# Two blocks of a top-k threshold search pass from a search on VectorE and ScalarE to one on ScalarE alone

## The chip, the cores and the metric

The kernel runs on one core of one Trainium2 chip. Its time is the device time of one execution in microseconds (us). The profile is of one execution and counts from the first instruction to the last (the span). Of the core's engines the text names TensorE (PE: matmuls; PEld: the loading of their weights), VectorE (DVE), ScalarE (ACT), GpSimd (POOL) and SyncE (SP), which issues most DMAs. PE, ACT, DVE, POOL and SP each take their own instructions in order.

## What is computed

One decoder layer on 1024 tokens of width 1024. Two branches read the same projection: an RWKV-7 recurrence (8 heads of 64) and a sparse attention in which an indexer picks for each query the 256 keys with the highest score. Their outputs are gated, added to the input, and followed by a SwiGLU block. The change is in the part that picks the keys:

```python
def one_block(args):                       # 8 blocks of 128 queries
    ...
    sc = jax.nn.relu(einsum('bqhd,bsd->bqhs', qib, k_idx))
    score = einsum('bqhs,bqh->bqs', sc, wib) * idx_scale
    score = jnp.where(causal, score, -jnp.inf)
    _, sel = lax.top_k(score, topk)        # topk = 256
    ...
    prob = jax.nn.softmax(logits_of_selected, axis=-1)
```

Block b has (b+1)*128 keys that a query may see. Blocks 0 and 1 see at most 256, so nothing is picked there. Blocks 2 to 7 have 384, 512, 640, 768, 896 and 1024 keys.

## The kernel before

**Order of work.** PE's instructions keep the order in which the program is written; those of the other engines are put in order when the kernel is built, earlier lines first where several could start, and later lines wherever an engine would else be idle. `fill` is a queue of generators of matmul work; `pump(n)` takes about n matmuls from it, and so the text of the program says which matmuls of the fill lie between those of the main work. `ticks(n, m)` spreads n such matmuls over m equal parts and takes one step of the generator `beside` after each part.

**Stages.** First the projections of the indexer, then `scores`: for each of blocks 2 to 7 the products on PE, a rectification on ACT (L970) and a weighted sum on DVE. Beside this and the first search PE takes the projections of the RWKV and attention inputs from `fill`. Then comes `rwkv` for four quarters q = 0 to 3 of 256 tokens. Beside q = 0 PE takes the projection of V and half of the gates, beside q = 1 the attention of blocks 0 to 3 (`attend(0)`) and the other gates, beside q = 2 and 3 the merge and the FFN of the first half of the tokens. After `rwkv` follows `attend(1)` for blocks 4 to 7, with the rest of the first half's FFN as fill, and then the second half's merge and FFN.

**The search.** `image` turns the scores into integers with the same order (L986, L987). `select` then finds for each query the 256th highest value by bisection: 16 steps on the upper 16 bits, a preparation (L1040 on ACT, L1042 on DVE, in pieces of up to 512), and 16 steps on the rest. Each step counts, for each block, how many values reach the threshold. A block is counted either on DVE (`is_ge` with a sum, L1015) or on ACT (`Sign` with a sum, L1018); the first `nv` of its `order` are DVE's. With `nv` above 0 the thresholds are moved by three small DVE instructions for all blocks together (L1020 to L1022), and with `nv` = 0 by two small ACT instructions for each block (L1026, L1027). At the end each block gets a mask `bias[b]`: a `Sign` on ACT (L1056), six DVE instructions (L1057 to L1062), and a copy on ACT (L1063).

There are two searches. The first is written behind the scores and handles blocks 5, 2 (DVE) and 4, 3 (ACT). The second (`LATE`, blocks 7 and 6, `nv` = 0) is the generator `beside`: its 16 steps, preparation, 16 steps and two masks make 35 steps, which `ticks` takes in 14, 4, 9 and 6 during the quarters of `rwkv` and in 2 at the end. The scores of `LATE` blocks are kept in tiles `kept` of their own (4 bytes a value), and their masks are written into the same memory; the other blocks have a mask tile of 2 bytes a value and scores in a pool that is closed before `rwkv`. The second search writes its unused result to `junkl`, the first to `junk`. In the second search the preparation and the masks take `tmp` tiles, of which there are four, in turn with everybody else: two for a mask, one for a piece of the preparation.

**Weights.** A weight tile is loaded by DMA into one of three `wst` tiles (from SP's queue, and during `rwkv` from ACT's), then split into a high part on ACT (L116) and a low part on DVE (L117), and multiplied in three terms (L149, L150, L154).

**GpSimd.** It issues the loads of q = 0 of `rwkv` (L566), those of `attend` (L1077 to L1105), and a few late ones. [...]

## Time and profile before

| what | value |
|---|---|
| median of 3 runs | 1708.05 us (1706.07 to 1708.38) |
| profiled execution, span | 1703.6 us |
| TensorE clock granted, mean | 0.996 of full |
| PE busy | 1683.7 us, 99% of the span, 10802 matmuls |
| PEld busy | 1417.2 us, 83% |
| DVE busy | 1182.2 us, 69% |
| ACT busy | 896.6 us, 53% |
| POOL busy | 96.6 us, 6% |

The profile gives the profiled execution its span and no time of its own beside it; the span is 4.45 us below the median of the runs, in which what lies before the first and behind the last instruction counts too. Matmuls overlap in the profile (one of 128x512 takes 0.39 us, and the next starts 0.23 us after it), so that PE is called busy also while it is a little held up. Views with stretches of the span give each engine's busy time inside them and, in brackets, the number of its instructions.

### The profile page before, as it was taken

The numbers are of one execution on the slowest core, as the hardware profiler recorded it, in microseconds if no ns is written. First come the engines' busy times: TensorE is split into PE (matmuls) and PEld (weight loads), VectorE is DVE, ScalarE is ACT, GpSimd is POOL, SyncE is SP. The second block draws the span as 40 slices with busy tenths as digits, with TensorE's granted clock in tenths as the row PEclk, the third lists the DMA queues.
The fourth block names the chain that finished last, engine by engine and source line by source line (L and its number), as shares of the span: only waits on it lengthen the run. The fifth ranks groups of instructions, "written<-read, shape, count | busy, mean of one in ns | idle before, by whom it ended". The sixth has DMA issues, their size and how long they took to land.

```text
span 1703.6 us, 28293 instructions
## 1 busy us (share of the span) xinstructions
PE 1683.7 (99%) x10802; PEld 1417.2 (83%) x10802; DVE 1182.2 (69%) x2305; ACT 896.6 (53%) x1727; POOL 96.6 (6%) x107
## 2 busy tenths in 40 slices
PE   9999999999999999999999999999999999999998
PEld 7888888878778777878787888888888899899998
DVE  6789989967467558957886655535564885775763
ACT  6366898463545788755334365533323544353452
POOL 0000000000021110000200210000100000000002
PEclk9999999999999999999999999999999999999999
DMA  5452334445357625653343633244455344524532
GB/s 215 162 154 79 108 99 151 131 126 172 106 168 211 175 95 169 205 175 108 106 136 98 211 126 118 80 150 161 160 179 180 112 161 133 176 100 142 168 112 99
DMA packets 142232, 243.58 MB, mean 143 GB/s; under 512 B 48865, under 2 KB 71073, under 8 KB 141969
## 3 DMA queue, kind: packets, MB, share of 16 engines
q1 hardware_dynamic: 119360, 170.76, 31.3%
q10 hardware_dynamic: 16128, 48.60, 8.7%
q0 software_dynamic: 6608, 22.42, 4.2%
q8 instruction: 85, 1.39, 0.3%
q14 instruction: 51, 0.41, 0.1%
HBM read 188.73 MB, written 53.00 MB: 142 GB/s over the span
## 4 chain that ended last, share of the span: by engine, by line
PE 92%; DVE 3%; ACT 2%; DMA 1%; issue 1%; POOL 1%; SPq 0%; ACTq 0%; DVEq 0%; POOLq 0%
PE acc L149 20%; PE acc L154 19%; PE acc L150 19%; PE acc L167 4%; PE mix L1617 3%; PE mix L1615 3%; PE mix L1614 3%; PE mix L1164 2%; PE mix L1154 2%; PE mix L968 2%; PE acc L424 1%; PE mix L1138 1%; PE mix L149 1%; PE acc L1617 1%; PE mix L150 1%; PE mix L154 1%
## 5 line engine op out<-in xcount | busy, mean ns | idle before, releaser
L117 DVE TENSOR_TENSOR wlo<-wst,whi 128x1024 fp32r<-128x1024 f32 (+1 forms) x203 | 249.0, 1228 | 175.3 <-PE acc L154 72.8
L116 ACT ACTIVATE whi<-wst 128x1024 fp32r<-128x1024 f32 (+1 forms) x203 | 212.3, 1048 | 185.8 <-PE acc L150 135.0
L149 PE MATMUL acc<-zhi,whi 128*128 128x512 f32 x400 | 158.8, 397 | 0.0
L150 PE MATMUL acc<-zlo,whi 128*128 128x512 f32 x400 | 156.1, 390 | 0.0
L149 PE MATMUL acc<-u1hi,whi 128*128 128x512 f32 x320 | 128.0, 400 | 0.0
L150 PE MATMUL acc<-u1lo,whi 128*128 128x512 f32 x320 | 125.3, 392 | 0.0
L149 PE MATMUL acc<-u0hi,whi 128*128 128x512 f32 (+1 forms) x320 | 122.8, 386 | 0.0
L150 PE MATMUL acc<-u0lo,whi 128*128 128x512 f32 (+1 forms) x320 | 121.3, 382 | 0.0
L154 PE MATMUL acc<-zhi,wlo 128*128 128x512 f32 x400 | 103.1, 395 | 0.0
L149 PE MATMUL acc<-fhi,whi 128*128 128x512 f32 x234 | 91.9, 393 | 0.6 <-ACT whi L116 0.5
L150 PE MATMUL acc<-flo,whi 128*128 128x512 f32 x234 | 91.1, 390 | 0.0
L149 PEld LDWEIGHTS acc<-zhi,whi 128*128 128x128 f32 x400 | 75.1, 188 | 16.9 <-issue 1.8
L150 PEld LDWEIGHTS acc<-zlo,whi 128*128 128x128 f32 x400 | 75.2, 188 | 14.7
L154 PEld LDWEIGHTS acc<-zhi,wlo 128*128 128x128 f32 x400 | 73.6, 188 | 15.6 <-issue 1.2
L154 PE MATMUL acc<-u1hi,wlo 128*128 128x512 f32 x320 | 82.1, 396 | 0.0
L154 PE MATMUL acc<-u0hi,wlo 128*128 128x512 f32 (+1 forms) x320 | 78.7, 384 | 0.0
L1018 ACT ACTIVATE junkl<-kept,z 128x1024 int8<-128x1024 int16 (+1 forms) x64 | 69.4, 1084 | 5.2 <-DVE kept L987 4.4
L149 PEld LDWEIGHTS acc<-u1hi,whi 128*128 128x128 f32 x320 | 60.1, 188 | 12.6 <-issue 0.9
L149 PEld LDWEIGHTS acc<-u0hi,whi 128*128 128x128 f32 x320 | 60.2, 188 | 11.9 <-issue 0.4
L154 PEld LDWEIGHTS acc<-u1hi,wlo 128*128 128x128 f32 x320 | 59.3, 189 | 12.7 <-issue 0.9
L150 PEld LDWEIGHTS acc<-u1lo,whi 128*128 128x128 f32 x320 | 60.2, 188 | 11.3
L150 PEld LDWEIGHTS acc<-u0lo,whi 128*128 128x128 f32 x320 | 60.2, 188 | 11.0
(457 smaller groups left out, 4037.8 us busy)
## 6 DMA issues: line engine op xcount, KB each, us to landing
wst<-in_w_ffn_in SPq DMA_DIRECT2D x72, 512.0 KB, 3.9
wst<-in_w_in ACTq DMA_DIRECT2D x36, 512.0 KB, 3.8
wst<-in_w_in SPq DMA_DIRECT2D x25, 512.0 KB, 4.2
wst<-in_w_fo SPq DMA_DIRECT2D x25, 512.0 KB, 3.4
h<-in_xT SPq DMA_DIRECT2D x32, 256.0 KB, 5.2
d_g<-tmp ACTq DMA_DIRECT2D x32, 256.0 KB, 3.1
k<-d_k POOLq DMA_DIRECT2D x16, 512.0 KB, 5.9
tmp<-d_g SPq DMA_DIRECT2D x32, 256.0 KB, 2.7
```

Source lines behind the costliest of these rows:

```text
L116: A.activation(hi, x, AF.Copy)
L117: V.tensor_tensor(lo, x, hi.bitcast(F32), op=ALU.subtract)
L149: T.matmul(ps, whi[:, wk + k, :], ahi[:, ak + k, tok], start=k == 0, stop=False)
L150: T.matmul(ps, whi[:, wk + k, :], alo[:, ak + k, tok], start=False, stop=False)
L154: T.matmul(ps, wlo[:, wk + k, :], ahi[:, ak + k, tok], start=False, stop=k == nk - 1)
L167: T.matmul(ps, w[:, k, :], a[:, k, tok], start=k == 0 and j == 0, stop=k == nk - 1 and j == 2)
L968: T.matmul(ps[:, :w], iq[:, h, :], ik[:, i, c:c + w], start=i == 0, stop=i == 1)
L1018: A.activation(junka[:, :n], y, AF.Sign, bias=z[:, i:i + 1], accum_out=cnt[:, i:i + 1])
L1154: T.transpose(ps[:, j * 128:(j + 1) * 128], L[:, (c + j) * 128:(c + j + 1) * 128], ident)
L1614: T.matmul(ps, whi[:, k, :], ahi[:, k, :], start=opens and k == 0, stop=False, skip_group_check=True)
L1615: T.matmul(ps, whi[:, k, :], alo[:, k, :], start=False, stop=False, skip_group_check=True)
L1617: T.matmul(ps, wlo[:, k, :], ahi[:, k, :], start=False, stop=k == 3, skip_group_check=True)
```

## The change

`LATE` becomes 7, 6, 5, 4 and the first search keeps blocks 3 and 2, block 3 on DVE and block 2 on ACT (`nv` = 1). Blocks 5 and 4 get `kept` tiles and lose their 2-byte mask tiles, and four blocks share the second search, which then has 37 steps: one more is taken in q = 3 and one more at the end. A padding tile at the end of the pool grows from 16 to 80 values, and the scratch area for the descriptors of GpSimd's DMAs is set to 8 KB.

```diff
-            ticks((209, 231, 281, 232)[q], (14, 4, 9, 6)[q])
+            ticks((209, 231, 281, 232)[q], (14, 4, 9, 7)[q])
...
             if q == 3:
-                ticks(62, 2)
+                ticks(62, 3)
...
-    LATE = [7, 6]
+    LATE = [7, 6, 5, 4]
...
-        bp.tile([128, 16], F32, name="edge")
+        bp.tile([128, 80], F32, name="edge")
...
-        order = [5, 2, 4, 3]
+        order = [3, 2]
         for b in order + LATE:
             image(scs[b], sp2.tile([128, (b + 1) * 128], I32, tag="im", name="im", bufs=2))
             pump(10)
...
-        for y in select(sp2, [scs[b] for b in order], order, 2, bias, *junk,
+        for y in select(sp2, [scs[b] for b in order], order, 1, bias, *junk,
                         lambda n: sp2.tile([128, S], BF16, tag="mk", name="mk", bufs=4)[:, :n]):
             pump((17, 18, 22)[y])
...
-    nc = bacc.Bacc("TRN2", target_bir_lowering=False, num_devices=1)
+    nc = bacc.Bacc("TRN2", target_bir_lowering=False, num_devices=1, dynamic_dma_scratch_size=8192)
```

## The prediction

> **What bounds the kernel now.** The page is read first, then the table of stretches over the stages that the change touches, then PE's waits in the worst of them.

> ```profile
> span 1703.6 us, 28293 instructions
> PE 1683.7 (99%) x10802; PEld 1417.2 (83%) x10802; DVE 1182.2 (69%) x2305; ACT 896.6 (53%) x1727; POOL 96.6 (6%) x107
> ```

> PE is busy for all but 19.9 us of the span, so no change to DVE or ACT can remove more than that, and a busy PE may still be a little held up. Where the missing time lies is seen in the stretches:

> ```profile
> 174.00:340.00 166.00, 166.00 (x734) 137.35 (x733) 153.23 (x388) 136.62 (x318) 1.50 (x2) 1.00 0.39 119
> 340.00:400.00 60.00, 59.76 (x356) 48.26 (x355) 39.78 (x83) 35.08 (x83) 5.62 (x2) 1.00 0.48 145
> 572.00:600.00 28.00, 26.26 (x362) 20.75 (x363) 9.76 (x29) 22.18 (x60) 1.96 (x3) 0.94 0.51 156
> 600.00:690.00 90.00, 85.22 (x712) 66.84 (x708) 67.22 (x140) 77.33 (x190) 10.18 (x6) 1.00 0.45 146
> 690.00:726.00 36.00, 35.86 (x158) 29.67 (x159) 34.33 (x86) 25.43 (x55) 0.00 (x0) 1.00 0.58 199
> 726.00:870.00 144.00, 142.05 (x1089) 115.08 (x1088) 109.92 (x226) 67.16 (x127) 13.05 (x5) 1.00 0.40 122
> 870.00:912.00 42.00, 41.92 (x454) 33.90 (x454) 25.87 (x54) 16.13 (x32) 0.00 (x0) 1.00 0.43 128
> 912.00:950.00 38.00, 38.00 (x288) 31.19 (x285) 30.86 (x56) 18.45 (x38) 4.61 (x4) 1.00 0.44 131
> 950.00:975.00 25.00, 25.00 (x119) 20.43 (x118) 11.56 (x18) 7.20 (x8) 4.56 (x7) 1.00 0.74 262
> ```

> The columns after the length are busy PE, PEld, DVE, ACT and POOL. From 174 to 340 both searches run (first search, and the first half of the second one), with DVE at 92% and ACT at 82%, and yet PE misses nothing. That it really runs at its pace there is seen in the chain of waits, where the last 8 of every 24 matmuls of a projection appear at even distance:

> ```profile
> 164.07 1.81 PE acc L154 x8
> ...
> 327.27 1.81 PE mix L154 x8
> ```

> 163.2 us are 30 times 5.44 us, 24 matmuls at 0.227 us each, without one late. PE's losses lie in quarter 1 of `rwkv`: 1.74 us from 572 to 600, 4.78 us from 600 to 690, where ACT is 86% busy, and 1.95 us from 726 to 870. So the stage that the change relieves has nothing to give, and the stage that it loads is the one where PE loses.

> **The change part by part.** PE's instructions and their order stay: neither `select` nor `ticks` issues a matmul, and `pump` and `ticks` take the same totals.

> Work of the second search on ACT:

> ```profile
> 564.00:726.00 162.00, 37.70 (x64) 0.99 0.50 160
> 174.00:340.00 166.00, 37.60 (x64) 1.00 0.39 119
> L1018 ACT ACTIVATE junkl<-kept,z 128x1024 int8<-128x1024 f32 x16 | 18.2, 1137 | 0.6 <-DVE kept L1042 0.6
> L1018 ACT ACTIVATE junkl<-kept,z 128x896 int8<-128x896 f32 x16 | 16.5, 1034 | 0.1
> L1018 ACT ACTIVATION_READ_ACCUMULATOR junkl<-kept,z 128x1 f32 x64 | 12.0, 188 | 0.0
> L1026 ACT ACTIVATE ge<-cnt,thr 128x1 f32<-128x1 f32 x64 | 16.2, 280 | 0.0
> L1027 ACT ACTIVATE z<-ge,z 128x1 f32<-128x1 f32 x64 | 16.8, 283 | 0.4 <-DVE W L763 0.3
> L1018 ACT ACTIVATE junk<-sc,z 128x640 bf16<-128x640 f32 x16 | 13.2, 822 | 7.9 <-DVE z L1022 7.8
> L1056 ACT ACTIVATE mk<-sc,ge 128x768 bf16<-128x768 f32 x1 | 0.9, 921 | 0.0
> L1056 ACT ACTIVATE mk<-sc,ge 128x384 bf16<-128x384 f32 x1 | 0.6, 601 | 0.0
> ```

> The first two rows are the counting of the second search (tile `junkl`) in its two halves: 16 steps in 37.6 us, 2.35 us a step. Its four instructions last 1137 + 1034 + 2*188 = 2547 ns, so 0.10 us is lost in overlap for each block. The two small ones take (16.2 + 16.8)/64 = 0.52 us for each block and step. A `Sign` of 768 takes 0.92 us (the mask's row), one of 640 0.82 us. Block 5 adds 0.92 + 0.19 - 0.10 + 0.52 = 1.53 us to a step, block 4 1.43: 2.96 us, or **47.4 us of ACT in each half**. The halves take 101 instead of 54 us.

> From 174 to 340 the first search gives work back:

> ```profile
> 174.00:340.00 166.00, 52.44 (x128) 54.82 (x128) 1.00 0.39 119
> L1015 DVE TENSOR_SCALAR_CACHE_REDUCE junk<-sc,z 128x768 bf16<-128x768 f32 x16 | 16.2, 1011 | 0.4
> L1015 DVE TENSOR_SCALAR_CACHE_REDUCE junk<-sc,z 128x384 bf16<-128x384 f32 x16 | 9.8, 610 | 0.3
> L1058 DVE TENSOR_TENSOR_SCAN sc<-mk 128x768 f32<-128x768 bf16 x1 | 1.8, 1752 | 0.0
> ```

> The first row is tile `junk`: 52.44 us on DVE (blocks 5 and 2), 54.82 on ACT (4 and 3). After the change ACT counts block 2: 32 * (0.60 + 0.19 - 0.10) = 22.1 us, 32.7 less. DVE counts block 3, 512 wide: a third of the way from 610 to 1011 ns is 744, with some 83 for reading the sum 0.83 us, 32 times 26.5 us, 25.9 less. The two masks and the two preparations that leave are some 3.9 and 2.8 us of ACT by the same rows. ACT holds 136.6 + 47.4 - 32.7 - 6.7 = **144.6 of 166 us, 87%**: the added first half fits where the old one did, before `rwkv`, beside projections that run at PE's pace, and if it doesn't it may stretch to 564, where the preparation begins. Value: nothing. Bounds: a gain of 0.24 us (all that 340 to 400 misses, should `rwkv`'s first elementwise work start earlier), a loss of about as much; I take -0.1.

> The second half starts behind the preparation, at about 572. There ACT is busy for 22.18 + 77.33 + 25.43 = 124.9 of the 154 us to 726, and the old half just ends. The added 47.4 us, and 2.8 of preparation, fall behind 726, where ACT is busy for 67.16 of 144. Filled to the 86% of 600 to 690, that stretch has room for 56.6 us, so the search ends at about 726 + 144*50.2/56.6 = **854**, before its masks are made (from 912 on in the trace). What does it cost PE that `Sign` stands in ACT's queue for another 128 us?

> ```profile
> 614.90 1.14 ACT L1018 ACTIVATE junkl<-kept,z 128x1024 int8<-128x1024 f32 x1
> ...
> 616.74 0.77 ACT L875 ACTIVATE UV<-mix 64x256 f32<-64x256 f32 x2
> ...
> 617.16 0.97 PE L884 MATMUL mix<-UV,NAT 128*64 128x64 f32 x16 [0.72 <-ACT UV L875]
> ...
> PE mix L1119 <- ACT x L593: 1.0, 1, 1.0
> PE mix L884 <- ACT UV L875: 0.7, 1, 0.7
> PE mix L1154 <- DVE mx L1121: 0.7, 1, 0.7
> PE mix L1154 <- ACT x L593: 0.3, 1, 0.3
> ```

> Here a `Sign` and an attention exponential stand ahead of the copy of UV, and PE waits 0.72 us. Of PE's 4.78 us from 600 to 690 2.0 name ACT. Low end: nothing, as from 690 to 726, where the search runs and PE misses 0.14 us. High end: all of 600 to 690, 4.78/90 = 0.053 us per us, over 128 us 6.8, less the 1.7 that these already miss: **+5.0**. Attention's work on ACT, which made the L593 and L1154 waits, is gone behind 690; the UV kind, 0.7 per 90 us, gives 1.0 over 128 us, the 2.0 give 2.8. I take **+1.5**. Each longer `Sign` also stands before weight loads that ACT's queue issues; three `wst` tiles, each worth 48 matmuls or 10.9 us of PE, cover a landing of 3.8:

> ```profile
> wst<-in_w_in ACTq DMA_DIRECT2D x36, 512.0 KB, 3.8
> k<-d_k POOLq DMA_DIRECT2D x16, 512.0 KB, 5.9
> q0 software_dynamic: 6608, 22.42, 4.2%
> 938.29 1.04 ACT L1056 ACTIVATE tmp<-kept,ge 128x896 bf16<-128x896 f32 x1 [2.07 <-DMA d_h<-tmp]
> ...
> 947.68 0.95 ACT L1063 ACTIVATE kept<-tmp 128x896 bf16<-128x896 bf16 x1 [1.27 <-DVE tmp L1062]
> ...
> 974.08 0.49 DVE L1141 CUSTOM_DVE_ANT_0 L<-mix,bias 128x320 f32<-128x320 f32 x1 [1.89 <-PE mix L1138]
> ```

> The two masks move from about 316 to 334 behind the old last one. Block 6 holds two of the four `tmp` tiles from 938.29 to 948.63, 10.3 us, and began 2.07 us late, since a `tmp` was still being stored to `d_h`. Blocks 5 and 4 are narrower, and blocks 6, 5 and 4 now share the last 62 matmuls. Their DVE work, dominated by the scan (1.75 us for block 5), is some 8 us in a stretch where DVE is busy for 68.3 of 105. Block 4 is made last and needed first, at 974.08. Two more masks, overlapped as far as the `tmp` tiles allow, end at about 960: 14 us to spare. Bounds 0 and +3.7 (below); I take +0.5.

> Scratch of 8 KB: POOL's queue carries 6608 packets in the whole run, and each load of `attend` is issued two blocks ahead. Nothing; at worst POOL once waits out a landing, +5.9. The padding costs nothing, a guess without a row. No DMA is added or moved, and SP's queue issues the same.

> [...]

> Sum: 1703.6 - 0.1 + 1.5 + 0.5 = 1705.5 us of span. The median of the runs lies 4.45 above the profiled span, so the forecast is **1710.0 us**, or 0.1% more. About 0.2%, 3.4 us, is what a measurement of this kernel can tell from no change.

> **The rivals.** *ACT as bound to 854* (slower): the second half makes 726 to 854 what 600 to 690 is. Its place is ACT's queue in quarters 2 and 3, its price +5.0, with the mask's 0.5 1713.6 us. It decides from the point where ACT is 86% busy there. For it speaks that the list of waits names ACT, against it that merge and FFN ask less of ACT than attention.

> *The `tmp` tiles* (slower): each of blocks 6, 5 and 4 holds two tiles for 10.3 us, while an FFN tile of 24 matmuls comes every 5.44. If they can't overlap, evictions fall 3 * 4.9 = 14.6 us behind; the two other `acc` banks cover 10.9. +3.7, with ACT's 1.5 1713.2 us. Against it speaks that PE misses nothing from 912 to 975 now.

> *PE hides it all* (no change): the change does only half of what it says, since the first half runs before `rwkv` anyway, and the second finds room. 1708 us.

> *The search leaves the worst stretch* (faster): the preparation now needs eight `tmp` tiles in turn, not four. If that pushes the second half's start from 571 beyond 690, 600 to 690 loses its `Sign`s and falls to the rate of 726 to 870: 1.95/144*90 = 1.2 instead of 4.78. -3.6: 1704.5 us. Against it: a wait for a few `tmp` is some us long, not 118.

> A variant rests on a held-up PE that is called busy. PEld is 137.35/166 = 82.7% busy in the projections and 66.84/90 = 74.3% from 600 to 690; at the same pace (82.7 - 74.3)/82.7*90 = 9.1 us would be lost there, not 4.78. If shorter `Sign`s (a mean of 0.98 instead of 1.09 us) and a new order halve this, -4.6: 1703.5 us. [...]

> **How the numbers follow.** Forecast 0.37 and "PE hides it all" 0.14, both within 0.2%: **same 0.51**. ACT as bound 0.22, `tmp` 0.08: **slower 0.30**. The search leaves 0.14, the held-up PE 0.05: **faster 0.19**. The range 1703.5 to 1715 takes in the two sides, and a little of POOL's wait; the forecast's own is 1708 to 1713.

> **What would show it.** `junkl` busy some 70 us (16 * 4.28) up to 340 and the rest from 572 to about 854; 174 to 340 with PE still full and DVE some 30 us less busy; PE missing about 3.5 instead of 1.95 us from 726 to 870; the last L1063 before 965. The prediction is wrong if PE misses over 6 us there, if L1138 waits for a mask, if the second half starts far from 572, or if 600 to 690 changes by over 2 us.

## The result, and the profile after

The changed kernel takes **1715.56 us** (median of 5 runs, 1713.98 to 1718.16), the kernel before 1706.07 us in the runs beside it (5 runs, 1701.35 to 1708.38): a ratio of 1.006, 95% interval 1.0041 to 1.0079, so 0.6% slower. The forecast was 1710.0 us and its range ended at 1715: the time lies outside. As a difference the miss is larger than it looks, since the forecast started from a median of 1708.05: +1.95 us was forecast, +9.5 us came.

The page of the changed kernel, span and engines:

```profile
span 1712.0 us, 28421 instructions
PE 1686.6 (99%) x10802; PEld 1419.0 (83%) x10802; DVE 1160.6 (68%) x2242; ACT 947.1 (55%) x1919; POOL 97.1 (6%) x107
```

PE has the same 10802 matmuls. The span grew by 8.4 us in two ways: PE stands still for 25.4 instead of 19.9 us (+5.5), and the same matmuls keep it busy for 2.9 us longer. Both are seen in the table of stretches, with the columns of the prediction's table (busy PE, PEld, DVE, ACT, POOL, then the granted clock of PE, the share of DMA and its GB/s):

```profile
174.00:340.00 166.00, 166.00 (x734) 137.43 (x734) 121.99 (x306) 143.31 (x374) 1.50 (x2) 1.00 0.42 132
564.00:572.00 8.00, 6.01 (x37) 4.74 (x36) 7.91 (x17) 4.91 (x9) 2.44 (x4) 1.00 0.84 215
572.00:600.00 28.00, 24.17 (x304) 19.39 (x303) 8.17 (x24) 22.69 (x63) 1.97 (x3) 0.82 0.40 115
600.00:690.00 90.00, 86.94 (x752) 68.03 (x751) 66.58 (x138) 76.40 (x194) 10.80 (x6) 1.00 0.45 142
726.00:870.00 144.00, 137.72 (x1062) 110.53 (x1061) 103.86 (x212) 102.58 (x238) 13.05 (x5) 1.00 0.41 125
912.00:950.00 38.00, 37.92 (x364) 30.59 (x363) 28.98 (x56) 18.07 (x38) 3.27 (x2) 1.00 0.38 119
```

The kernel before has no loss from 564 to 572:

```profile
564.00:572.00 8.00, 8.00 (x48) 6.47 (x47) 6.70 (x13) 6.00 (x13) 2.44 (x4) 1.00 0.63 151
```

From 174 to 340 PE is as full as it was, with DVE 31 us less busy. The loss lies elsewhere: 1.99 us from 564 to 572 (0 before), 3.83 from 572 to 600 (1.74 before, and the clock is 0.82 instead of 0.94), 6.28 from 726 to 870 (1.95 before). From 600 to 690 PE even misses less (3.06 us, 4.78 before). The list of PE's waits from 560 to 870 (us in total, times, longest) names what ended them:

```profile
PE mix L812 <- ACT TZ L794: 4.4, 3, 3.8
PE mix L662 <- ACT nrT L656: 2.3, 1, 2.3
PE mix L1154 <- DVE mx L1121: 2.0, 1, 2.0
```

The kernel before has the third at 0.7 and the other two not in its list. At L812 its PE stands still too, for 1.7 us, and the profile names nothing that it waits for:

```profile
PE mix L812 <- issue: 1.7, 1, 1.7
```

TZ and nrT are small tiles of `rwkv` that ACT copies out of one product of PE for the next one. Each wait is read in the order in which an engine took its instructions (start, duration, engine and operation, and in brackets the idle time ahead). First the wait at 568.8, on DVE and then on PE:

```profile
567.41 2.64 DVE L1042 TENSOR_TENSOR kept<-tmp,kept 128x512 f32<-128x512 f32 x5
569.98 0.67 DVE L1121 CUSTOM_DVE_ANT_0 L<-mix,bias 128x512 f32<-128x512 f32 x1
```

```profile
570.81 0.63 PE L1154 MATMUL mix<-kc,L 128*128 128x128 f32 x4 [1.99 <-DVE mx L1121]
```

Five pieces of the preparation (L1042) stand in a row ahead of the attention's pass L1121, for which PE waits. Then the longest wait, behind the copies of TZ on ACT:

```profile
578.02 1.13 ACT L1018 ACTIVATE junkl<-kept,z 128x1024 int8<-128x1024 f32 x1
...
579.27 0.38 ACT L794 ACTIVATE TZ<-mix 32x256 f32<-32x256 f32 x1
579.67 1.04 ACT L1018 ACTIVATE junkl<-kept,z 128x896 int8<-128x896 f32 x1
...
580.90 0.92 ACT L1018 ACTIVATE junkl<-kept,z 128x768 int8<-128x768 f32 x1
...
582.00 0.81 ACT L1018 ACTIVATE junkl<-kept,z 128x640 int8<-128x640 f32 x1
...
583.86 0.38 ACT L794 ACTIVATE TZ<-mix 32x256 f32<-32x256 f32 x1
```

The same place in the kernel before:

```profile
579.53 1.57 ACT L794 ACTIVATE TZ<-mix 32x256 f32<-32x256 f32 x4
```

Before, the four copies run back to back in 1.57 us. Now the second copy starts 4.59 us after the first, because almost a whole step of the search (three Signs and their small operations) was put between them. PE waits 3.8 us. Last, the wait for nrT, on ACT and on PE:

```profile
827.38 0.92 ACT L1018 ACTIVATE junkl<-kept,z 128x768 int8<-128x768 f32 x1
...
828.81 0.81 ACT L1018 ACTIVATE junkl<-kept,z 128x640 int8<-128x640 f32 x1
...
829.62 0.36 ACT L656 ACTIVATE nrT<-mix 16x256 fp32r<-16x256 f32 x1
```

```profile
830.03 0.73 PE L662 MATMUL mix<-nrT,ind 16*128 16x256 f32 x4 [2.26 <-ACT nrT L656]
```

All three are work of the second search (its preparation, then its steps) that stands ahead of work PE is waiting for.

### The profile page after: what moved, and what is told of

It is laid out like the page before. It is cut to its first block, busy times and chain, and to the rows that moved or that the text cites. A ratio compares the mean times of both kernels' runs of the same rounds, so it can differ in the third digit from the quotient of the medians.

```text
span 1712.0 us, 28421 instructions
## 1 busy us (share of the span) xinstructions
PE 1686.6 (99%) x10802; PEld 1419.0 (83%) x10802; DVE 1160.6 (68%) x2242; ACT 947.1 (55%) x1919; POOL 97.1 (6%) x107
## 3 DMA queue, kind: packets, MB, share of 16 engines
q0 software_dynamic: 6608, 22.42, 4.3%
## 4 chain that ended last, share of the span: by engine, by line
PE 85%; DVE 6%; ACT 5%; DMA 2%; issue 1%; POOL 1%; SPq 0%; ACTq 0%; DVEq 0%; POOLq 0%
PE acc L149 18%; PE acc L154 18%; PE acc L150 18%; PE acc L167 3%; PE mix L1614 3%; PE mix L1617 3%; PE mix L1615 3%; PE mix L968 2%; PE mix L1164 2%; PE mix L1154 1%; DVE wlo L117 1%; PE mix L1138 1%; PE acc L424 1%; ACT junkl L1018 1%; PE mix L149 1%; PE acc L1617 1%
## 5 line engine op out<-in xcount | busy, mean ns | idle before, releaser
L150 PE MATMUL acc<-zlo,whi 128*128 128x512 f32 x400 | 156.1, 390 | 0.0
L1018 ACT ACTIVATE junkl<-kept,z 128x1024 int8<-128x1024 int16 (+7 forms) x128 | 125.0, 977 | 1.8 <-DVE kept L987 1.3
L150 PE MATMUL acc<-u1lo,whi 128*128 128x512 f32 x320 | 125.5, 392 | 0.0
L150 PE MATMUL acc<-u0lo,whi 128*128 128x512 f32 (+1 forms) x320 | 121.3, 382 | 0.0
L154 PE MATMUL acc<-zhi,wlo 128*128 128x512 f32 x400 | 103.1, 395 | 0.0
L150 PE MATMUL acc<-flo,whi 128*128 128x512 f32 x234 | 91.1, 389 | 0.0
L150 PEld LDWEIGHTS acc<-zlo,whi 128*128 128x128 f32 x400 | 75.2, 188 | 14.7
L154 PEld LDWEIGHTS acc<-zhi,wlo 128*128 128x128 f32 x400 | 73.6, 188 | 15.6 <-issue 1.2
L154 PE MATMUL acc<-u1hi,wlo 128*128 128x512 f32 x320 | 82.3, 397 | 0.0
L154 PE MATMUL acc<-u0hi,wlo 128*128 128x512 f32 (+1 forms) x320 | 78.6, 384 | 0.0
L154 PEld LDWEIGHTS acc<-u1hi,wlo 128*128 128x128 f32 x320 | 59.4, 190 | 12.7 <-issue 0.9
L150 PEld LDWEIGHTS acc<-u1lo,whi 128*128 128x128 f32 x320 | 60.4, 189 | 11.4
L150 PEld LDWEIGHTS acc<-u0lo,whi 128*128 128x128 f32 x320 | 60.2, 188 | 11.0
## 6 DMA issues: line engine op xcount, KB each, us to landing
wst<-in_w_ffn_in SPq DMA_DIRECT2D x72, 512.0 KB, 3.8
wst<-in_w_in ACTq DMA_DIRECT2D x36, 512.0 KB, 4.2
wst<-in_w_in SPq DMA_DIRECT2D x25, 512.0 KB, 3.5
wst<-in_w_fo SPq DMA_DIRECT2D x25, 512.0 KB, 3.7
k<-d_k POOLq DMA_DIRECT2D x16, 512.0 KB, 6.0
```

The source lines that it names most:

```text
L150: T.matmul(ps, whi[:, wk + k, :], alo[:, ak + k, tok], start=False, stop=False)
L154: T.matmul(ps, wlo[:, wk + k, :], ahi[:, ak + k, tok], start=False, stop=k == nk - 1)
L1018: A.activation(junka[:, :n], y, AF.Sign, bias=z[:, i:i + 1], accum_out=cnt[:, i:i + 1])
```

## The experiments

Since PE takes the same matmuls in the same order in all the kernels of this table, the start of each matmul can be subtracted from the start of the same matmul in the profile of the kernel before. The growth of that lag, in us, is given here by stretches of the before time; it adds waits and slower matmuls together. A column ends at the time at its head. Each row is one profiled execution; the verdicts below go by the times of all runs. The first 20 us are left out: the kernel before spent 3.4 us of them at half clock (8.9 to 12.4), the changed kernel none, and it is 2.3 us ahead there.

```
                 20-560  -600   -640   -690   -726   -770   -860
after             -0.5   +6.8   -1.5   +0.6    0.0   +2.7   +3.4
e1_scratch        +0.5   -1.6    0.0   +0.2    0.0   -0.1    0.0
e2_relief         -0.5   +1.1    0.0   -0.2    0.0   +4.4    0.0
e3_noprep         -0.5   +1.0   +5.6   +3.8   +1.6   +0.5   -0.5
e4_hold           -0.1   +1.9   -1.8   +3.9    0.0   +7.4   +4.4
e5_double         +2.2   +0.6   -1.1   +1.0    0.0   +2.2   +0.9
e6_half           -0.5   +6.6   -1.5   +2.0    0.0   +0.1    0.0
e8_before_apart  +26.8   -1.1   -1.8   +2.4    0.0   +0.4    0.0
e9_add            +0.1   +1.9   +4.4   +3.6   +1.6   +0.1   -0.5
e10_thin          +0.3   -0.7   +5.3   +0.8    0.0   +3.7    0.0
e13_count         +1.1   +1.7   -1.5   +2.0    0.0   +3.0   -0.4
e16_shift         +0.2   -2.2    0.0    0.0    0.0   +2.8    0.0
e18_one           +0.1   -0.2   -0.5   +0.5    0.0   +2.5    0.0
```

The rows of `e1_scratch` and `e16_shift` show how little one execution can say. By their traces PE, ACT and DVE take the instructions of the kernel before in the same order in both (the step that the edit of `e16_shift` moves is built back to its old place), and yet they differ from it by 1.6 and 2.2 us from 560 to 600, and `e16_shift` by 2.8 us from 726 to 770. So the +2.7 of the changed kernel from 726 to 770, which is there in `e18_one` and `e2_relief` too, is not shown to be the change's.

**The parts that were thought free.** The kernel before with the scratch alone (`e1_scratch`):

```diff
+    nc = bacc.Bacc("TRN2", ..., num_devices=1, dynamic_dma_scratch_size=8192)
```

> The kernel before with the 8 KB scratch as its only edit; each engine's instructions and their order stay. Theory (the loss is ACT work of the second search standing ahead of RWKV's copies): within 0.2% of the kernel before, PE's losses by stage as before (4.78 us from 600 to 690, under 2.5 from 726 to 870). Rival (the smaller scratch holds up GpSimd's DMAs): the loads of the attention come late, and the kernel is some us slower.

1707.22 us against 1706.3; ratio 1.0003 (0.9991 to 1.0015). The scratch is free.

The kernel before with the relief alone: blocks 5 and 4 leave the first search and join no other (`e2_relief`).

```diff
-        order = [5, 2, 4, 3]
-        for b in order + LATE:
+        order = [3, 2]
+        for b in order + [5, 4]:
+            V.memset(bias[b], 0.0) if b > 3 else None
+        for b in order + LATE:
```

> The kernel before with blocks 5 and 4 taken out of the first search and put nowhere: their masks are zero, so their share of the top-k is left out. It shows what the relief of the first stage is worth by itself. Theory: PE has nothing to win there, so the span falls by 0 to 0.5 us against the kernel before, and PE's start times stay within 1 us of it up to the end. Rival (the losses come from the new order of the first stage, not from the added ACT work): 4 us or more slower.

1707.69 us in one run. The 33 us of DVE and 31 of ACT that are not done from 174 to 340 buy nothing. That PE's start times would stay within 1 us did not hold: +1.1 and +4.4 us arose behind 560, far from the relieved stage.

**Taking suspects away from the changed kernel.** Without the preparation's pieces for blocks 5 and 4 (`e3_noprep`):

```diff
-        for i, x in enumerate(xs):
+        for i, x in enumerate(xs if nv else xs[:2]):
```

> The changed kernel without the preparation of blocks 5 and 4 for the second 16 steps (four pieces on ACT and four on DVE), so these two blocks are searched on in unprepared values. Theory: of the 6.3 us that PE loses from 565 to 585 against the kernel before, the 2.2 at about 571 go (PE waited for an exponential and a copy that stood behind four pieces waiting for temporary tiles); the loss at the TZ copies and those behind 726 stay: 1 to 3 us faster than the changed kernel. Rival (the whole loss from 565 to 585 is the Sign step between the TZ copies): no gain.

1714.26 us in one run. The wait at 571 is gone as expected, and the time hardly moves: PE now waits at 604 and 696 (2.2 us each, the one for `rhs`, L863, the other for an input of the merge, L1313). Two things came otherwise than expected: the wait for TZ falls to 1.3 us as well, and from 726 to 860 nothing is lost. The added preparation thus does more than hold up one pass on DVE. Without it the first Sign of the second half starts at 568.27, and the step is nearly over when the copies of TZ come up; with it that Sign starts at 578.02, beside them.

```profile
568.27 1.15 ACT L1018 ACTIVATE junkl<-kept,z 128x1024 int8<-128x1024 f32 x1 [0.60 <-DVE kept L1042]
...
579.83 1.17 ACT L794 ACTIVATE TZ<-mix 32x256 f32<-32x256 f32 x3
```

With the second half held back until the last copy of TZ in quarter 1 (`e4_hold`; `hold[0]` is that copy, and the built order may put the step's instructions only behind it):

```diff
-            ticks((209, 231, 281, 232)[q], (14, 4, 9, 7)[q])
+            ticks((209, 231, 281, 232)[q], (14, 4, 10, 7)[q])
...
-            next(beside[0], None)
+            with tc.issue_after(hold[0].ins) if (n, i) != (231, 3) and (count.append(0) or len(count) == 19) else nullcontext(): (n, i) != (231, 3) and next(beside[0], None)
```

> The changed kernel with the first step of the second half held until ACT has issued the last TZ copy of quarter 1; it is taken in quarter 2 instead, the rest as it was. Theory: PE's wait for the TZ copies (3.8 us) goes, with the 2.2 at about 571 left: 3 to 4.5 us faster than the changed kernel, unless the shift of the remaining steps puts a like wait elsewhere. Rival (PE waits there because of what precedes, an instruction fetch or the preparation): under 1 us.

1719.92 us in one run. The loss at 580 went, and behind 726 more came than had gone. The granted clock stands at 0.95 in nearly all of this execution (a mean of 0.944), but PE took the same 734 matmuls in these 166 us as in the kernel before at 1.00, so that doesn't explain the time:

```profile
174.00:340.00 166.00, 166.00 (x734) 137.47 (x733) 122.47 (x306) 143.87 (x376) 1.51 (x2) 0.95 0.43 132
```

It is one run, but no sign of a gain.

Preparation later, and the second half held as well (`e11_both`, with counts 14, 3, 10, 7):

> The changed kernel with the preparation taken later in quarter 1 (at the last of three parts instead of the third of four) and the second half held until the last TZ copy of quarter 1: the two places at which PE waits from 565 to 585 are changed together. Theory: these 6.3 us go and the half clock behind them; what is lost behind 726 stays: 4 to 8 us faster than the changed kernel. Rival (a step that is moved finds another copy to hold up): under 2 us faster.

1721.16 us, ratio 1.0089 (1.0073 to 1.0105): no better than the change. Only 8 of the 16 steps in the second half (`e6_half`, the other eight left out):

> The changed kernel with the second half of the second search cut from 16 steps to 8, so that the last bits of the thresholds are left out. Theory: the search is over at about 690 us, and the 6.1 us that PE loses behind 726 against the kernel before go, while the loss from 565 to 600 stays: 4 to 7 us faster than the changed kernel. Rival (what is lost behind 726 comes from the masks or from other tiles): no gain there.

1714.74 us, 1.0053 (1.0038 to 1.0068). In the profiled execution the lag behind 726 went and that up to 600 stayed; but that execution was a quick one (1711.9 us), and by the median only 0.8 us came back, where 4 to 7 were expected. With the second search's steps pinned to quarters 0, 2 and 3, so that quarter 1 has none (the 18th step, which is the first of the second half, and the first ones of quarters 2 and 3 only behind a copy of their own quarter, L742), in the changed kernel (`e7_apart`, counts 22, 0, 8, 4) and in the kernel before (`e8_before_apart`, counts 27, 0, 5, 1):

```diff
-            ticks((209, 231, 281, 232)[q], (14, 4, 9, 7)[q])
+            ticks((209, 231, 281, 232)[q], (22, 0, 8, 4)[q]) if q != 1 else pump(231)
```

> The changed kernel with the steps of the second half put where ACT has room: preparation and five steps in quarter 0 behind its transposed copies (NAT), eight in quarter 2 and three in quarter 3, each group held until that quarter's last NAT copy is issued; none in quarter 1, beside the attention. The same work in all. Theory (the place of the steps counts): PE loses 0 to 3 us against the kernel before from 565 to 870 instead of 13, and the time comes within 0.2% of the kernel before or below. Rival (the amount of ACT work counts): it stays 5 us or more above the kernel before.

> The kernel before (blocks 7 and 6) with its second half's steps put in the same places: preparation and ten steps in quarter 0, five in quarter 2, one in quarter 3, none beside the attention. Theory: PE loses less than before from 570 to 690, where the Signs stood among attention's and RWKV's copies: 2 to 6 us faster than the kernel before. Rival (the losses there are attention's own): within 2 us of it.

1751.23 us (1.0262, 1.0245 to 1.0278) and 1729.73 us (1.0139, 1.0123 to 1.0155). Both were expected near or below the kernel before. PE's waits in the two:

```profile
PE mix L812 <- ACT TZ L794: 39.2, 4, 20.7
```

```profile
PE mix L812 <- ACT TZ L794: 22.5, 3, 18.1
```

Here is the mechanism undiluted: steps crowded into quarter 0 are put ahead of the copies of TZ, and one wait lasts 20.7 us. It happens with two blocks as with four. The second run says too that the two-block search isn't what makes PE lose from 560 to 690 in the kernel before: pinned out of there, it won only 0.5 us.

**Adding the suspect to the kernel before.** Each Sign of the second half issued twice (`e5_double`; the two blocks then keep ACT counting for 75 us from 560 to 870, the changed kernel's four blocks 68.5):

```diff
-                        A.activation(junka[:, :n], y, AF.Sign, ...)
+                        for _ in range(1 if nv or y.dtype != F32 else 2): A.activation(junka[:, :n], y, AF.Sign, ...)
```

> The kernel before, with each Sign of the second half of the second search (blocks 7 and 6) issued twice with the same result: about 36 us more of ACT work there, with the first search, the masks, the tiles and the preparation untouched. Theory (more Signs ahead of RWKV's copies in ACT's queue are the loss): 4 to 9 us slower than the kernel before, lost between 570 and 870 us. Rival (the loss comes from the preparation, the masks, the tiles or the first search): within 2 us of the kernel before.

1708.55 us, 1.0008 (0.9993 to 1.0023). **The time of Signs costs next to nothing here**: at most 0.23% by the interval. Then two further blocks, parts of the kept ones, counted in the second half beside the old two, with thresholds of their own that nobody reads (`e9_add` 768 and 640 wide, `e10_thin` 16 wide both, `e18_one` a single one of 16; the thresholds' tiles grow by as many columns):

```diff
-        yield from search(xs)
+        yield from search(xs + ([] if nv else [xs[0][:, :768], xs[1][:, :640]]))
```

> The kernel before, its first search, masks, tiles and preparation untouched, with two more blocks counted in the second half of the second search (768 and 640 wide, on the data of blocks 7 and 6, their results unused): steps of four blocks as in the changed kernel. Theory (a step of four blocks has twice as many instructions ready at any time, so longer runs of them stand ahead of RWKV's copies, and PE's waits are long enough for its clock to be halved): 5 to 9 us slower than the kernel before, lost from 575 to 870, though doubling the Signs of two blocks cost 2 us. Rival (the relief of the first search, the preparation and the tiles are what cost): within 3 us of the kernel before.

> As the run with two blocks added, but these two are 16 wide, so that a step has the same number of instructions and about 1.4 us less of work. Theory with weight on the length of the run of instructions: 1 to 4 us slower than the kernel before. With weight on their number: as slow as the run with the two wide blocks, 5 to 9 us.

> The kernel before with one further block of 16 columns counted in the second half (three chains; nobody reads its result). If the loss grows with the chains, it lies between e1_scratch (no chain added) and e10_thin (two added): 1708 to 1712 us. If it is the arrangement, it may come out anywhere from 1705 to 1717 us.

`e9_add`: 1715.34 us, 1.0061 (1.0044 to 1.0078): a loss of the same size is back, without the first search, preparation, masks or scratch of the change. It sits where that of `e3_noprep` sits, the kernel with the same steps of four blocks and no added preparation; PE's two longest waits in `e9_add` are the same two:

```profile
PE mix L872 <- DVE rhs L863: 2.4, 2, 2.2
PE acc L149 <- DVE tmp L1313: 1.9, 1, 1.9
```

`e10_thin`: 1713.86 us, 1.005 (1.0035 to 1.0065), though its Signs last 0.3 us. `e18_one`: 1707.91 us, 1.0003 (0.999 to 1.0016). In `e10_thin` the longest wait is the one for `rhs` again:

```profile
608.23 0.90 PE L872 MATMUL mix<-rhs,TT 64*64 64x64 f32 x10 [2.18 <-DVE rhs L863]
```

```profile
607.19 0.69 DVE L913 TENSOR_TENSOR yb<-yb,yrs 128x512 f32<-128x512 f32 x1 [1.51 <-POOL yrs L912]
607.90 0.28 DVE L863 TENSOR_TENSOR rhs<-mix,rhs 64x128 f32<-64x128 f32 x1
```

PE waits for the last of four additions L863, which was put behind L913, and L913 waits for GpSimd. In the kernel before the four run together, ahead of all that:

```profile
603.30 1.21 DVE L863 TENSOR_TENSOR rhs<-mix,rhs 64x128 f32<-64x128 f32 x4
...
607.63 0.69 DVE L913 TENSOR_TENSOR yb<-yb,yrs 128x512 f32<-128x512 f32 x1 [1.84 <-POOL yrs L912]
```

The search has no instruction on DVE at all in its second half: the work added on ACT moved what stands in DVE's queue. The same four additions are torn apart in the same way in `e3_noprep` and `e9_add`, and in no other run does PE wait for them that long. Whether the number of instructions does it or the number of chains (the steps of one block are a chain, each needs the one before; those of different blocks don't), `e13_count` asked: Signs and small operations of the two old blocks issued twice, so a step has the instructions of four blocks in two chains.

```diff
                         A.activation(ge[:, c], cnt[:, c], AF.Sign, bias=thr[:, c])
+                        if ys[0].dtype == F32:
+                            A.activation(top[:, c], ge[:, c], AF.Identity, scale=..., bias=z[:, c])
+                            A.activation(ge[:, c], cnt[:, c], AF.Sign, bias=thr[:, c])
```

> The kernel before, with every Sign and both small operations of the second half issued twice (the second small result goes to a tile that nobody reads): a step of two blocks has 4 Signs and 8 small operations, as many as a step of four blocks, but in two chains instead of four. If the number of ScalarE instructions costs, it comes out like e10_thin and e9_add: 1713 to 1716 us, ratio 1.004 to 1.006. If it is the two further independent chains (work that is always ready to be put ahead of a copy), it comes out like e5_double: 1706 to 1709.5 us, ratio 0.999 to 1.002.

1710.16 us, 1.0016 (1.0003 to 1.0029): nearer to `e5_double` than to `e10_thin`, and its interval ends below the latter's. Here four chains cost more than as many instructions in two.

**Other arrangements.** Is it bad luck of one arrangement? The kernel before with its late blocks swapped (`e15_swap`) and with a step moved from quarter 2 to 3 (`e16_shift`), the changed kernel with its blocks reversed (`e17_after_swap`), and with a step handed out in two halves of two blocks (`e14_pairs`):

```diff
-    LATE = [7, 6]
+    LATE = [6, 7]
```

```diff
-            ticks((209, 231, 281, 232)[q], (14, 4, 9, 6)[q])
+            ticks((209, 231, 281, 232)[q], (14, 4, 8, 7)[q])
```

```diff
-    LATE = [7, 6, 5, 4]
+    LATE = [4, 5, 6, 7]
```

```diff
-            ticks((209, 231, 281, 232)[q], (14, 4, 9, 7)[q])
+            ticks((209, 231, 281, 232)[q], (28, 7, 18, 13)[q])
...
+                    if not nv and i % 2:
+                        for j in (i - 1, i):
+                            c = slice(j, j + 1)
...
+                        if i < nb - 1:
+                            yield 0
```

> The kernel before with the two late blocks in the other order (6, then 7): same instructions, same two chains, another arrangement. If only further chains cost, it stays within 0.2% of the kernel before: 1704 to 1709.5 us. If any rearrangement costs what the change costs, 1711 to 1717 us.

> The kernel before with one step of the second half moved from the third to the fourth quarter of RWKV (ticks 8 and 7 instead of 9 and 6): no work added. By the theory of the chains 1704 to 1709.5 us; if any rearrangement costs, 1711 to 1717 us.

> The changed kernel with its four late blocks in the reverse order (4, 5, 6, 7): same work, four chains, another arrangement. By the theory of the chains it loses about as much as the changed kernel: 1712 to 1719 us. If the loss is that of one unlucky arrangement, another one may give it back: 1706 to 1711 us.

> The changed kernel with a step of the second search handed out in two halves, blocks 7 and 6 and then blocks 5 and 4, with twice as many ticks over the same code: same instructions, same four chains. If whole runs of four Signs and eight small operations ahead of a copy are what costs, half runs leave PE's waits behind L794 and L656 under 2 us and most of the loss goes: 1707 to 1711 us. If it is the number of instructions in ScalarE's queue, or the chains being ready at all, it stays at 1713 to 1717 us.

The two edits of the kernel before cost nothing: 1.0008 (0.9991 to 1.0025) and 1.0 (0.9983 to 1.0017). Only `e15_swap` is another arrangement, though; `e16_shift` came out as the kernel before. Those of the changed kernel gain nothing: 1715.33 us, 1.0052 (1.0033 to 1.007), and 1717.96 us, 1.0062 (1.0041 to 1.0082). In `e14_pairs` the wait for TZ fell from 3.8 to 1.0 us, as the halved runs of Signs should make it, and the wait for L1121, in front of which the preparation stood, grew in its place to 4.5 us:

```profile
PE mix L1156 <- DVE mx L1123: 5.1, 2, 4.5
...
PE mix L812 <- ACT TZ L794: 1.0, 1, 1.0
```

Its lines are two higher: L1156 and L1123 are L1154 and L1121. So the runs of whole steps explain one wait, not the loss. Last, three blocks late and three in the first search (`e12_three`):

```diff
-    LATE = [7, 6, 5, 4]
+    LATE = [7, 6, 5]
...
-        order = [3, 2]
+        order = [4, 3, 2]
```

> Half of the change: the second search takes blocks 7, 6 and 5, the first keeps 4, 3 and 2 (block 4 on VectorE). Theory (length of a step and of the preparation): between the two kernels, 2 to 6 us slower than the kernel before. Rival (all or nothing at one place): as the kernel before or as the changed one.

1719.87 us, 1.0088 (1.0073 to 1.0103): not between the two kernels but at least as slow as the changed one, with a wait of 3.4 us for TZ and two for nrT. It is no clean test of three blocks, though: alone among these kernels it has another order of PE's matmuls too (736 of 10802 places). No version tried beats the kernel before.

## Why the prediction was wrong

**What held.** PE is the bound, and the relieved stage had nothing to give (`e2_relief`). The first half of the search fits before `rwkv`: PE stays full up to 340, ACT is busy for 143.31 us (forecast 144.6) and DVE for 31.2 less (some 30). Scratch and masks cost nothing: PE misses 0.08 of 38 us from 912 to 950. The last mask's copy, in the group of L1063, starts at 959.4; it is the narrowest, 0.74 us, and so ends at 960.1 (about 960 was forecast):

```profile
L1063 ACT ACTIVATE kept<-tmp x4: 737/898/1047, 904.3 to 959.4; 128x1024 bf16<-128x1024 bf16 x1, 128x896 bf16<-128x896 bf16 x1, 128x768 bf16<-128x768 bf16 x1, 128x640 bf16<-128x640 bf16 x1
```

The counting of the second search, tile `junkl`, lies where it was forecast to lie:

```profile
174.00:340.00 166.00, 64.97 (x122) 1.00 0.42 132
...
572.00:600.00 28.00, 8.57 (x16) 0.82 0.40 115
830.00:845.00 15.00, 4.29 (x8) 1.00 0.26 79
845.00:870.00 25.00, 0.00 (x0) 1.00 0.46 130
```

It ends by 845, and 854 was forecast. Its second half begins at 578 instead of 572.

**What failed is the step "What does it cost PE that `Sign` stands in ACT's queue for another 128 us?", valued at +1.5 (0 to +5.0).** Three things in it were wrong.

- *The place.* The prediction added work only behind 726 and left 564 to 726 as it was. But a step is four blocks long from the first one on, and the first one met the copies of TZ: 6.8 us of lag arose from 560 to 600, against nothing forecast. Behind 726 the expected kind of loss came too: 6.28 us missing, over the 6 that the prediction named as a sign of being wrong, and 4.3 more than before, of which 1.0 came in `e16_shift` too, with the old order (2.91 us missing), and 1.6 in `e18_one` (3.53).
- *The preparation.* It was priced as 2.8 us of ACT. Its additions on DVE (L1042) were not counted in their queue, and five of them in a row made the wait of 1.99 us. It also moved the first Sign of the second half to 578, beside the copies of TZ. `e3_noprep` took the first wait away and left 1.3 us of the second, and the lag from 560 to 600 fell from 6.8 to 1.0 us, so the preparation's part there is shown. That the time hardly fell shows that it isn't the cause of the whole: with the added preparation the changed kernel waits at TZ, without it at `rhs`.
- *The measure.* The price went by the time of Signs, at a rate per us. `e5_double` adds more of that time than the change and costs 1.0008; `e10_thin` adds hardly any and costs 1.005. The runs fit a price that goes by how many independent chains ACT is given to choose from when its queue is put in order, and by which copy then ends behind them; that is a reading of them and not shown.

In the sum a term is missing besides: behind the wait of 3.8 us PE's granted clock was 0.50 for 10.2 us, where the kernel before has 3.4 us at 0.50 (last section), which is part of the +2.9 us of busy PE. The prediction had a row that shows it (0.94 from 572 to 600) and didn't use it. The base was loose as well: of the 4.45 us that were added to the span, 2.0 lie outside it (the changed kernel's profiled execution took 1713.98 us with a span of 1712.0), and the rest is that the profiled execution of the kernel before was a quick one. That moves the forecast time, not the forecast difference.

The nearest rival was "ACT as bound to 854", 1713.6 us: right in its kind, an ACT queue that delays PE, and wrong in its place. The held-up PE and "the search leaves the worst stretch" found no support, though 600 to 690 did miss 1.7 us less.

**What stays open.** Every form with four chains in the second half lost 0.5 to 0.9% (pinned, 2.6%), and two chains, swapped or doubled, lost 0 to 0.16% (pinned, 1.4%). One thin chain more was free; three full blocks were not, but there PE's order changed too. So the law of the count is open. The places of the loss are not random: the three forms without the added preparation (`e3_noprep`, `e9_add`, `e10_thin`) all wait 2.2 us for `rhs`, and the changed kernel, `e6_half` and `e17_after_swap` all wait 3.8 us for TZ. That argues for the order that is built, in which more ready work makes it likelier that something stands ahead of a needed copy. It isn't the amount of reordering: by the traces, and leaving the search's own work aside, 50 of DVE's instructions leave their old order in `e18_one` and 56 in `e15_swap`, both free, and 45 in `e10_thin`. What counts is which ones. The order was seen at the places quoted; that it explains the rest is argued, not shown.

## What to carry to other kernels

Work moved "beside" a full engine is not priced by its duration: look up which short copies the full engine waits for, and ask what may now stand ahead of each in its queue, on every engine that the moved work uses. The number of independent chains can matter more than the time: here four cost 0.5 to 0.9%, and as many instructions in two 0.16%. Taking one cause of a wait away is not enough either: without the added preparation nearly the whole loss came at other places. With PE at 99%, relief of the other engines bought nothing.

## What was not expected of the hardware

```profile
579.70:583.10 3.40, 0.81 (x5) 0.32 (x3) 0.00 (x0) 3.40 (x10) 0.00 (x0) 1.00 0.02 4
583.10:593.30 10.20, 8.96 (x104) 7.62 (x105) 1.58 (x6) 9.91 (x26) 1.20 (x2) 0.50 0.05 17
```

At the wait of 3.8 us, from 583.1 on, PE ran at 0.50 for 10.2 us; a matmul of 128x512 (L150) took 0.63 us at 588.88 and 0.39 at 579.48, before the wait. Half of the 8.96 us that it was busy for in them, 4.5 us, is an estimate of what the clock cost there. The kernel before has 3.4 us at half there, behind a wait of 1.74:

```profile
585.80:589.20 3.40, 3.40 (x24) 2.58 (x24) 1.01 (x4) 3.10 (x9) 1.19 (x2) 0.50 0.13 27
```

In `e10_thin` 6.8 us at half came at the wait of 2.18 us:

```profile
603.80:607.20 3.40, 2.07 (x12) 1.20 (x10) 1.76 (x8) 3.10 (x14) 1.66 (x1) 1.00 0.02 5
607.20:610.60 3.40, 2.37 (x14) 1.87 (x14) 0.97 (x2) 2.25 (x8) 0.00 (x0) 0.50 0.00 0
610.60:614.00 3.40, 3.40 (x24) 2.51 (x22) 1.22 (x1) 1.32 (x3) 0.00 (x0) 0.50 0.22 25
```

But the wait of 2.26 us at 828 in the changed kernel was followed by none:

```profile
825.40:828.80 3.40, 2.21 (x10) 1.54 (x10) 1.85 (x3) 3.40 (x6) 0.00 (x0) 1.00 0.51 154
828.80:832.30 3.50, 2.27 (x15) 2.03 (x16) 3.36 (x7) 2.37 (x9) 0.00 (x0) 1.00 0.44 152
```

So the length of the wait alone doesn't tell whether the clock falls: it fell at 1.74 and 2.18 us, and not at 2.26. PE's busy time in these stretches doesn't either: in `e18_one` the half clock came behind a stretch with more work than those at 828, though of small matmuls (72 of them):

```profile
578.80:582.20 3.40, 2.45 (x72) 1.75 (x73) 0.00 (x0) 3.28 (x8) 0.00 (x0) 1.00 0.09 30
582.20:585.60 3.40, 3.40 (x20) 2.79 (x19) 1.15 (x4) 1.89 (x7) 0.00 (x0) 0.51 0.02 5
```

What decides it was not shown.

Runs of one kernel differ along with the granted clock. In 80 runs of the kernel before, taken beside the experiments (one of 8016 us left out), the mean time was 1703.1 us where the mean granted clock was 0.999 (10 runs), 1706.7 at 0.997 (30) and 1711.8 at 0.994 (5). That is about 1.8 us for each 0.001, and 3.4 us at half clock, the stretch of the kernel before, lower the mean over its span by 0.001. At 0.996 the kernel before took 1709.7 us (10 runs) and the changed one 1713.98 and 1715.56: about 5 us of its loss remains at an equal clock. The 0.95 of `e4_hold` is another thing: its matmuls kept their pace (734 from 174 to 340, as at 1.00).
